# A decoder step on one core: convolution taps taken first, the convolution's scaling taken beside the input projection, three more weight tiles kept longer

## The chip, the cores and the metric

One Trainium2 chip, of which the kernel uses one core. The metric is the time of the device in microseconds (us). The profile is one execution on the chip; its rows name the engines: PE (matrix products), PEld (their weight loads), DVE (element by element), ACT (functions and copies), POOL (which here mostly issues transfers) and SP (which only issues transfers).

## The reference

One layer of a decoder trunk over 320 tokens (256 of a prompt, 8 sequences of 8 samples), in float32. Only what lies around the change is kept:

```python
ada = jax.nn.silu(c) @ w_ada + b_ada                 # (9, 2048) @ (2048, 12288)
sh1, sc1, g1, sh2, sc2, g2 = jnp.split(ada[:, None, :], 6, axis=-1)
h = _layer_norm(x) * (1.0 + sc1) + sh1
proj = h @ w_in                                      # (320, 2048) @ (2048, 7168)
u_s  = proj[..., :1024]                              # input of the S5 scan
u_c2 = proj[..., 1024:3072]                          # a * sigmoid(b): input of the convolution
gates = jax.nn.sigmoid(proj[..., 3072:])
y_s = S5 scan of u_s, then GELU, then two products (w_s5_val, w_s5_gate)
v = depthwise convolution, 31 taps, of a * sigmoid(b)
v = silu(_layer_norm(v, conv_ln_g, conv_ln_b)) @ w_conv_pw
x = layer_norm(alpha * x + g1 * ((g_s * y_s + g_c * v) @ w_out)); then the mixture of experts
```

## The kernel before

**Matrix products in three parts.** A weight is read in float32 into a tile `raw` (4 buffers of 128x1024, 512 KB each), and `split` makes of it `whi` (ACT, a rounding cast, L555) and `wlo` (DVE, `raw - whi`, L556). PE then multiplies `whi` with the high and the low part of the activations and `wlo` with the high part (`mm3`). A `gemm` makes 256 columns of the output in chunks of 512 KB of weights; one chunk is 24 matmuls of 320 columns (`acc<-h_hi,whi`, `acc<-h_lo,whi`, `acc<-h_hi,wlo`).

**The stages.** First `w_ada`, 1024 columns at a time (`ada_set`), which has the nine condition vectors `scT` as stationary operand; each step is a group of four matmuls that read two tiles, written `adp<-raw,scT` or `adp<-rawu,scT`. Four sets must be done before `h` is; beside them the layer norm of `x` and `s5_setup`, the tables of the S5 scan and small constants, go on, and `k_outer` begins the input projection's first 768 columns. Next the rest of the input projection: 2 x 4 gemms for the convolution's input (`ev_ua`, `ev_ub`) and then 16 gemms for the gates (`ev_g`), 64 chunks. Then `w_conv_pw` in 16 chunks (`acc<-vhl,whi`), the two products of the S5 branch, `w_out`, and the experts.

**What is done beside.** After every chunk `run_main` gives its side generators a budget: 2100 ns to the S5 scan `s5()` and 1700 ns to `conv()` followed by `conv_norm()`, and one step of the other `w_ada` sets (`ada_rest`). A generator's `yield` says what its piece costs. The convolution runs on PE as matmuls over `wide` (taps spread to a diagonal) and leaves `vf`; `conv_norm` sums `vf` and the squares (matmuls with `ones`), and makes the factor `rs` with `rstd_` (L318 to L324: a square root on ACT, a reciprocal and four more steps on DVE). `conv_out` multiplies `vf` by it (L910), takes silu (L911) and splits the result into `vhl` (L914, L915), which is the right operand of the `w_conv_pw` product. What is left of `conv_norm`, and all of `conv_out`, is run off between the last gate chunk and the first chunk of `w_conv_pw`.

**Weight tiles.** `ada_load` puts every other tile of `w_ada` into one of three extra tiles, `rawu` (two, in the buffer that `vf` takes later) and `rawc` (in the one that `wide` takes later), as long as the list `more` is not empty; `more.clear()` (L637) ends that before the last four `k_outer`. All loads of weights go through SP's queue in program order; a load waits there until its tile is free. S5's operands `Bs`, `us` and the convolution's windows `up_d` go through POOL's queue.

**Taps.** In `s5_setup` the weights of the convolution (31x1024) are brought from columns to rows by 128 small matmuls (`tpp<-kc,cwn`) that share the only `tpp` buffer of PSUM with all transposes.

The order of instructions on each engine is made by a scheduler that goes by data, buffers and priorities.

Of the kernel before, what the change touches and what calls it, by code (L numbers as in the profile page):

```python
# [9 lines left out]
F32 = mybir.dt.float32  # L10
F32R = mybir.dt.float32r
# [3 lines left out]
OP = mybir.AluOpType  # L15
AX = mybir.AxisListType.X
# [8 lines left out]
T = SEQ + NB * TS  # L25
NS = 1 + NB
DS = 1024
# [4 lines left out]
CW = 31  # L32
# [120 lines left out]
def build(tc, A, O):  # L153
    nc = tc.nc
    V, S, GP, PE, SY = nc.vector, nc.scalar, nc.gpsimd, nc.tensor, nc.sync
# [16 lines left out]
    cmr2, pr2 = pool(name="pr2", bufs=1, side="right")  # L172
    cma, pa = pool(name="pa", bufs=1)
# [7 lines left out]
    def tpp(name="tpp"):  # L181
        return pp.tile([128, 512], F32, name=name, tag="tpp", bufs=1)
# [4 lines left out]
    def mm(out, l, r, a, b, skip=True):  # L187
        return PE.matmul(out, lhsT=l, rhs=r, start=a, stop=b, skip_group_check=skip)  # L188

    tt, ts, stt = V.tensor_tensor, V.tensor_scalar, V.scalar_tensor_tensor  # L190
# [5 lines left out]
    ident = kc[:, C_ID:C_ID + 128]  # L196
# [12 lines left out]
    cwS = p0.tile([128, 8, 4, 8], F32, name="cwS", tag="cwT")  # L209
# [28 lines left out]
    def x_load():  # L238
        for i, (t0, n) in enumerate(TOK):
            if i < 2:  # L240
                SY.dma_start(out=xt[i], in_=A["x_prompt"][0, t0:t0 + n])
            else:
                SY.dma_start(out=xt[i][:n], in_=A["x_sample"].rearrange("b s d -> (b s) d"))
# [4 lines left out]
    ps = tpp()  # L248
# [81 lines left out]
    def ln0():  # L330
        st = stg("st")
        mv = stg("mv")
        for i, (t0, n) in enumerate(TOK):
            for c in range(4):
                V.bn_stats(st[:n, 24 * i + 6 * c:24 * i + 6 * c + 6], xt[i][:n, 512 * c:512 * c + 512])
            V.bn_aggr(mv[:n, 2 * i:2 * i + 2], st[:n, 24 * i:24 * i + 24].rearrange("p (c s) -> p c s", s=6))
            rstd_(mv[:n, 2 * i + 1:2 * i + 2], mv[:n, 16 + i:17 + i], mv[:n, 8 + i:9 + i])
            ts(xt[i][:n], xt[i][:n], mv[:n, 2 * i:2 * i + 1], mv[:n, 8 + i:9 + i], op0=OP.subtract, op1=OP.mult)

            stt(mv[:n, 24 + i:25 + i], mv[:n, 2 * i + 1:2 * i + 2], ALPHA, mv[:n, 8 + i:9 + i],  # L340
                op0=OP.mult, op1=OP.mult)
        yield
        for k in range(KT):
            ps = s5p()
            for i, (t0, n) in enumerate(TOK):
                PE.transpose(ps[:, t0:t0 + n], xt[i][:n, 128 * k:128 * k + 128], ident[:n, :n])
            S.copy(xnT[k // 8][:, k % 8, :], ps[:, :T])
            yield
        ps = tpp()
        for i, (t0, n) in enumerate(TOK):  # L350
            mm(ps[:, t0:t0 + n], bc(mv[:n, 24 + i:25 + i], [n, 128]), ident[:n, :n], True, True)
        V.tensor_copy(sdb, ps[:, :T])
        yield
# [35 lines left out]
    def s5_setup():  # L389
# [129 lines left out]
        ps = tpp()  # L519
        PE.transpose(ps[:, :64], vn[:64, :128], ident[:64, :64])  # L520
        V.tensor_copy(vT, ps[:, :64])
        cwn = pr2.tile([32, DS], F32, name="cwn", tag="Wb")
        GP.dma_start(out=cwn[:CW], in_=A["conv_w"][0])
        ps = tpp()
        pick = ident[:CW, 0:32].rearrange("p (r s) -> p s r", s=4)
        for c in range(8):
            for j in range(4):
                x = 32 * c + 8 * j
                for s in range(4):
                    mm(ps[32 * s:32 * s + 32, x:x + 8], cwn[:CW, 128 * c + 32 * j:128 * c + 32 * j + 32], pick[:, s, :],  # L530
                       True, True)
            yield 350
        V.tensor_copy(cwS.rearrange("p c j r -> p (c j r)"), ps[:, :256])
        V.tensor_reduce(oneh, ident.rearrange("p (a c) -> p c a", a=4), axis=AX, op=OP.add)
        yield 700

        h0 = p0.tile([128, 2, NB, NQ], F32, name="h0", tag="h0")
# [26 lines left out]
    def gemm(wv, c0, nk, xh, xl, evac):  # L564

        pss = []

        def load(k0):
            raw = raw_tile()
            SY.dma_start(out=raw.rearrange("p (k m) -> p k m", k=4), in_=wv[:, k0:k0 + 4, c0:c0 + 256])  # L570
            return split(raw, 1024)

        def prod(k0, hi, lo):
            if not pss:
                pss.extend(acc() for _ in range(2))
            for k4 in range(4):
                k = k0 + k4
                for m in range(2):
                    c = 256 * k4 + 128 * m
                    mm3(pss[m][:, :T], hi[:, c:c + 128], lo[:, c:c + 128], xh(k), xl(k), k == 0, k == nk - 1)  # L580
            if k == nk - 1:
                for m in range(2):
                    evac(c0 // 128 + m, pss[m][:, :T])

        for k0 in range(0, nk, 4):
            yield load, prod, k0
# [24 lines left out]
    def k_outer(k):  # L611
# [4 lines left out]
        for m in range(6):  # L616
            mm3(first[m][:, :T], hi[:, 128 * m:128 * m + 128], lo[:, 128 * m:128 * m + 128],
                hh[0](k), hh[1](k), k == 0, k == KT - 1)

    setup, norm = Side(s5_setup()), ln0()  # L620
    for q in range(4):
        for i, _ in enumerate(ada_set([D + 512 * q, 512 * q])):
            if q == 0:
                if i == 2:
                    x_load()
                if i == 3:
                    bias_rows()
                    next(norm)
                if 6 <= i < 15:
                    next(norm, None)  # L630
                    next(norm, None)
                setup.give(800)
            else:
                if i % 4 == 3 and i < 16:
                    k_outer(4 * q - 4 + i // 4)
                setup.give(1100)
    more.clear()  # L637
    for k in range(12, 16):
        k_outer(k)
    setup.flush()  # L640
# [209 lines left out]
    vv = {}  # L850
# [26 lines left out]
                yield 2000  # L877

    def conv_norm():
        yield 8000  # L880
        GP.dma_start(out=O["conv_p"][0, 0], in_=e_d[0:30])
        GP.dma_start(out=O["conv_s"][0, :, CW - 1 - TS:CW - 1], in_=e_d[30:94].rearrange("(b t) c -> b t c", b=NB))
        ps = s5p()
        for c in range(8):
            mm(ps[:, :T], ones, vf[:, c, :], c == 0, c == 7)
        yield 4000
        mu = stg("cmu")[:, :T]
        ts(mu, ps[:, :T], 1.0 / DS, None, op0=OP.mult)
        ps = s5p()
        for c in range(8):  # L890
            tt(vf[:, c, :], vf[:, c, :], mu, op=OP.subtract)
            sq = stg("csq")[:, :T]
            S.activation(sq, vf[:, c, :], AF.Square)
            yield 450
            mm(ps[:, :T], ones, sq, c == 0, c == 7)
        yield 1500
        va, tm = stg("cva")[:, :T], stg("ctm")[:, :T]
        rs = wide.rearrange("p j r x -> p (j r x)")[:, :T]
        ts(va, ps[:, :T], 1.0 / DS, None, op0=OP.mult)
        rstd_(va, tm, rs)  # L900
        yield 4500
        vv["rs"] = rs

    def conv_out():
        rs = vv["rs"]
        v_ = pa.tile([128, 2, 8, T], F32R, name="vhl", tag="H1")
        vv["hi"], vv["lo"] = v_[:, 0], v_[:, 1]
        for c in range(8):
            v = vf[:, c, :]
            tt(v, v, rs, op=OP.mult)  # L910
            S.activation(v, v, AF.Silu, bias=vT[:, 24 + c:25 + c], scale=vT[:, 16 + c:17 + c])  # L911
            yield 450
            hi, lo = vv["hi"][:, c, :], vv["lo"][:, c, :]
            S.copy(hi, v)  # L914
            tt(lo, v, hi.bitcast(F32), op=OP.subtract)  # L915
            yield 450

    ahead, due = [], []
# [1 line left out]
    def run_main(gens, sides=(), extra=None, before=None):  # L920


        def last():
            if ahead:
                prod, k0, hl, fn, sd, ev = ahead.pop()
                if fn:
                    fn()
                due.extend(later)
                later.clear()
                prod(k0, *hl)  # L930
                while due:
                    due.pop(0)()
                for x, ns in sd:
                    x.give(ns)
                if ev:
                    ev.give(1.0)

        for g in gens:
            for load, prod, k0 in g:
                hl = load(k0)  # L940
                last()
                ahead.append((prod, k0, hl, before, sides, extra))
                before = None
        if not gens:
            last()
# [29 lines left out]
            tt(x[o:o + 32], psg[r], x[r].bitcast(F32), op=OP.subtract)  # L975
        yield

    PACE = dict(s5=2100, conv=1700)
    def steps(g, cost):
        for _ in g:  # L980
            yield cost
# [13 lines left out]
    for i in range(4):  # L995
        run_main([gemm(w_in, 1024 + 256 * i, KT, *hh, ev_ua), gemm(w_in, 2048 + 256 * i, KT, *hh, ev_ub)], SD, ada_rest,
                 (lambda: side.g.append(s5())) if i == 0 else None)
    run_main([gemm(w_in, 3072 + 256 * i, KT, *hh, ev_g) for i in range(16)], SD, ada_rest,
             lambda: cside.g.extend((conv(), conv_norm())))


# [1280 lines left out]
```

## Time and profile before

| | us |
|---|---|
| median of 3 runs (1692.36 to 1695.34) | 1693.14 |
| the profiled execution | 1690.03 |
| its span | 1688.2 |
| PE busy | 1483.2 (88%) |
| DVE busy | 881.6 (52%) |
| ACT busy | 552.8 (33%) |
| mean granted clock of PE | 0.94 |

The stages in the trace: `w_ada` and setup 0 to 157 us, the first columns of the input projection to 179, the convolution's input and the gates to 708, `w_conv_pw` to 813, S5's products and `w_out` to about 1200, the experts to the end. Busy times are sums over an engine's instructions; what counts for the change is where PE stands idle and who ends that.

### The profile page before, as it was taken

What the parts mean: (1) busy time and instruction counts of PE and PEld (TensorE: products, weight loads), DVE (VectorE), ACT (ScalarE), POOL (GpSimd) and SP (SyncE); (2) the same over time, 40 slices, a digit from 0 to 9 for tenths busy, and PEclk for the clock granted to TensorE, in tenths of its full rate; (3) what the DMA queues carried; (4) which work ended last, traced back from release to release, by engine and by line L of the source; (5) the groups of instructions that cost most, each with busy time, mean ns of one, the idle gap of its engine ahead of it and who ended that gap; (6) DMA issues with size and microseconds to landing.
All of it is one profiled execution on the core that took longest, in us unless ns stands there. A gap on an engine that the chain in (4) does not pass through costs nothing. (4 is left out here: it accounts for less than half of the span.)

```text
span 1688.2 us, 28087 instructions
## 1 busy us (share of the span) xinstructions
PE 1483.2 (88%) x10731; PEld 1029.6 (61%) x10731; DVE 881.6 (52%) x1724; ACT 552.8 (33%) x960; POOL 248.6 (15%) x419
## 2 busy tenths in 40 slices
PE   4767988998998899949999999989889998969894
PEld 1444877877786777838899988848423332323331
DVE  5744347666744853695455554463531533424365
ACT  1312433342243234333343433331222423232434
POOL 3021312123223322011100000000200000010013
PEclk9887989999999999979999999988979999989997
DMA  9896999789688886637776645465799799999992
GB/s 287 273 340 221 283 276 240 232 222 260 183 251 202 207 235 206 183 126 235 242 255 221 210 136 170 154 231 208 293 406 412 299 412 402 412 365 412 412 410 73
DMA packets 214899, 447.39 MB, mean 265 GB/s; under 512 B 23811, under 2 KB 134067, under 8 KB 206732
## 3 DMA queue, kind: packets, MB, share of 16 engines
q1 hardware_dynamic: 179572, 395.65, 67.5%
q0 software_dynamic: 29168, 43.15, 11.1%
q10 hardware_dynamic: 6016, 6.70, 1.3%
q8 instruction: 87, 1.43, 0.4%
q14 instruction: 56, 0.46, 0.1%
HBM read 425.53 MB, written 21.77 MB: 265 GB/s over the span
## 5 line engine op out<-in xcount | busy, mean ns | idle before, releaser
L556 DVE TENSOR_TENSOR wlo<-raw,whi 128x1024 fp32r<-128x1024 f32 (+1 forms) x196 | 239.5, 1222 | 313.3 <-ACT whi L555 302.7
L555 ACT CAST whi<-raw 128x1024 fp32r<-128x1024 f32 (+1 forms) x196 | 201.9, 1030 | 419.7 <-PE acc L188 244.8
L188 PE MATMUL acc<-h_hi,whi 128*128 128x320 f32 x864 | 275.5, 322 | 14.0 <-ACT whi L555 11.7
L188 PE MATMUL acc<-h_lo,whi 128*128 128x320 f32 x864 | 272.3, 317 | 0.0
L188 PE MATMUL acc<-h_hi,wlo 128*128 128x320 f32 x864 | 259.0, 320 | 7.4 <-DVE wlo L556 7.1
L188 PEld LDWEIGHTS acc<-h_hi,whi 128*128 128x128 f32 x864 | 166.8, 194 | 41.3 <-ACT whi L555 21.3
L188 PE MATMUL up<-ring,xg 128*32 128x512 f32 x1344 | 181.6, 621 | 7.4 <-PEq L2197 6.5
L188 PEld LDWEIGHTS acc<-h_hi,wlo 128*128 128x128 f32 x864 | 161.8, 194 | 27.3 <-DVE wlo L556 13.2
L188 PEld LDWEIGHTS acc<-h_lo,whi 128*128 128x128 f32 x864 | 167.3, 194 | 2.6 <-issue 2.1
L188 PE MATMUL adp<-raw,scT 128*32 128x512 f32 x672 | 117.2, 673 | 31.5 <-DMA raw<-in_w_ada 31.4
L188 PEld LDWEIGHTS up<-ring,xg 128*32 128x32 f32 x1344 | 43.2, 115 | 100.4 <-issue 85.2
L188 PE MATMUL pd<-ring,aT 128*32 128x512 f32 (+1 forms) x688 | 98.2, 679 | 5.9 <-DVE aT L1870 5.9
L1708 DVE TENSOR_TENSOR x1tok<-x1tok,acc 128x512 f32<-128x512 f32 x80 | 51.8, 684 | 62.7 <-PE acc L188 62.4
L1926 ACT COPY z<-pd 32x512 f32<-32x512 f32 (+1 forms) x92 | 53.1, 577 | 89.0 <-PE pd L188 85.3
L188 PE MATMUL acc<-m_hi,whi 128*128 128x320 f32 x256 | 81.4, 319 | 0.0
L188 PE MATMUL acc<-m_lo,whi 128*128 128x320 f32 x256 | 80.0, 314 | 0.0
L188 PE MATMUL acc<-y_hi,whi 128*128 128x320 f32 x256 | 79.0, 311 | 0.0
L188 PE MATMUL acc<-y_lo,whi 128*128 128x320 f32 x256 | 78.6, 309 | 0.0
L188 PE MATMUL acc<-m_hi,wlo 128*128 128x320 f32 x256 | 78.2, 317 | 0.0
L188 PE MATMUL acc<-y_hi,wlo 128*128 128x320 f32 x256 | 74.7, 311 | 0.0
L188 PE MATMUL acc<-vhl,whi 128*128 128x320 f32 x256 | 57.3, 318 | 13.3 <-ACT vhl L914 12.9
L1609 DVE COPY xg<-XS 128x512 f32 x34 | 14.5, 428 | 81.2 <-PE up L188 78.4
(689 smaller groups left out, 2554.6 us busy)
## 6 DMA issues: line engine op xcount, KB each, us to landing
raw<-in_w_ada SPq DMA_DIRECT2D x128, 512.0 KB, 5.4
ring<-in_moe_w_up SPq DMA_DIRECT2D x120, 512.0 KB, 11.3
ring<-in_moe_w_gate SPq DMA_DIRECT2D x120, 512.0 KB, 10.5
ring<-in_moe_w_down SPq DMA_DIRECT2D x60, 1024.0 KB, 11.3
raw<-in_w_in SPq DMA_DIRECT2D x100, 512.0 KB, 4.9
raw<-in_w_ada SPq DMA_DIRECT2D x80, 256.0 KB, 5.5
raw<-in_w_out SPq DMA_DIRECT2D x32, 512.0 KB, 4.5
rawu<-in_w_ada SPq DMA_DIRECT2D x32, 256.0 KB, 5.4
```

The costliest lines, as they stand in the source:

```text
L188: return PE.matmul(out, lhsT=l, rhs=r, start=a, stop=b, skip_group_check=skip)
L555: S.copy(hi[:, :n], raw_ap)
L556: tt(lo[:, :n], raw_ap, hi[:, :n].bitcast(F32), op=OP.subtract)
L1609: state[g % 2] = (V.tensor_copy if g % 2 == 0 else S.copy)(xg[:, :, 32 * g:32 * g + 32], XS[:, :, bass.ds(off, 32)])
L1708: tt(x, x, o, op=OP.add)
L1926: S.copy(zs[q * ng + nb][0][s0:s0 + m_], pd[m_ * q:m_ * q + m_])
```

## The change

Three edits. The load of the convolution's weights and the 128 small matmuls on them leave `s5_setup` and stand in a function `taps()`, called at the third step of the first `w_ada` set; their tile is one of the `whi` buffers instead of the `Wb` buffer. `more.clear()` stands after the eight gemms `ev_ua`, `ev_ub`, so that `ada_rest` uses the three extra tiles there. The multiplication by `rs` and the silu go from `conv_out` to the end of `conv_norm`, whose first `yield` is 3000 instead of 8000, and the convolution's side is given 1900 instead of 1700 per chunk.

```diff
@@ s5_setup
-        cwn = pr2.tile([32, DS], F32, name="cwn", tag="Wb")
-        GP.dma_start(out=cwn[:CW], in_=A["conv_w"][0])
-        ps = tpp()
-        pick = ident[:CW, 0:32].rearrange("p (r s) -> p s r", s=4)
-        for c in range(8):
...
-            yield 350
-        V.tensor_copy(cwS.rearrange("p c j r -> p (c j r)"), ps[:, :256])
-        V.tensor_reduce(oneh, ident.rearrange("p (a c) -> p c a", a=4), axis=AX, op=OP.add)
@@ before the first ada_set
+    cwn = pa.tile([32, DS], F32, name="cwn", tag="whi", bufs=2)
+    GP.dma_start(out=cwn[:CW], in_=A["conv_w"][0])
+    def taps():
+        ps = tpp()
...
                 if i == 2:
                     x_load()
+                    taps()
...
-    more.clear()
     for k in range(12, 16):
         k_outer(k)
@@ conv_norm
-        yield 8000
+        yield 3000
...
         rstd_(va, tm, rs)
         yield 4500
-        vv["rs"] = rs
-
-    def conv_out():
-        rs = vv["rs"]
-        v_ = pa.tile([128, 2, 8, T], F32R, name="vhl", tag="H1")
-        vv["hi"], vv["lo"] = v_[:, 0], v_[:, 1]
         for c in range(8):
             v = vf[:, c, :]
             tt(v, v, rs, op=OP.mult)
             S.activation(v, v, AF.Silu, bias=vT[:, 24 + c:25 + c], scale=vT[:, 16 + c:17 + c])
             yield 450
-            hi, lo = vv["hi"][:, c, :], vv["lo"][:, c, :]
-            S.copy(hi, v)
-            tt(lo, v, hi.bitcast(F32), op=OP.subtract)
+
+    def conv_out():
+        v_ = pa.tile([128, 2, 8, T], F32R, name="vhl", tag="H1")
+        vv["hi"], vv["lo"] = v_[:, 0], v_[:, 1]
+        for c in range(8):
+            S.copy(vv["hi"][:, c, :], vf[:, c, :])
+            tt(vv["lo"][:, c, :], vf[:, c, :], vv["hi"][:, c, :].bitcast(F32), op=OP.subtract)
             yield 450
@@
-    PACE = dict(s5=2100, conv=1700)
+    PACE = dict(s5=2100, conv=1900)
@@ main loop
     for i in range(4):
         run_main([gemm(w_in, 1024 + 256 * i, ...ev_ua), gemm(w_in, 2048 + 256 * i, ...ev_ub)], SD, ada_rest, ...)
+    more.clear()
     run_main([gemm(w_in, 3072 + 256 * i, KT, *hh, ev_g) for i in range(16)], SD, ada_rest,
              lambda: cside.g.extend((conv(), conv_norm())))
```

**Place 1: the taps.** PE's order at the end of the `w_ada` stage of before: transposes for the S5 tables (L507, L520), the taps, two and one more groups on `w_ada`, and the first product on `h`.

```order
L507 MATMUL tpp<-kc,cN 128x128 x4
L520 MATMUL tpp<-kc,misc 128x64
L188 MATMUL tpp<-kc,cwn 32x8 x128
L188 MATMUL adp<-rawu,scT 32x512
L188 MATMUL adp<-raw,scT 32x512 x2
L188 MATMUL adp<-rawu,scT 32x512
L188 MATMUL adp<-rawc,scT 32x512
L188 MATMUL adp<-raw,scT 32x512 x2
L188 MATMUL adp<-rawc,scT 32x512
L546 MATMUL tpp<-kc,misc 128x128 x4
L188 MATMUL adp<-raw,scT 32x512 x4
L188 MATMUL tpp<-pair,ae 128x64 x8
```

The same place after the change (L533 is L546 of before); the taps are gone and the groups on `w_ada` stand one by one between the transposes, and half of `tpp<-pair,ae` goes ahead of the last group.

```order
L507 MATMUL tpp<-kc,cN 128x128 x4
L188 MATMUL adp<-rawu,scT 32x512
L188 MATMUL adp<-raw,scT 32x512 x2
L188 MATMUL adp<-rawu,scT 32x512
L507 MATMUL tpp<-kc,cN 128x128 x4
L520 MATMUL tpp<-kc,misc 128x64
L533 MATMUL tpp<-kc,misc 128x128 x4
L188 MATMUL adp<-rawc,scT 32x512
L188 MATMUL adp<-raw,scT 32x512 x2
L188 MATMUL adp<-rawc,scT 32x512
L188 MATMUL tpp<-pair,ae 128x64 x4
L188 MATMUL adp<-raw,scT 32x512 x4
```

PE's order at the beginning of the program after the change, from its fourth row; in before the rows without `cwn` stood there alone. 18 of the taps now stand between the first and the second group on `w_ada`, and 110 between the second and the third.

```order
L188 MATMUL adp<-rawu,scT 32x512
L188 MATMUL adp<-raw,scT 32x512 x2
L188 MATMUL adp<-rawu,scT 32x512
L397 MATMUL tpp<-kc,misc 128x96
L188 MATMUL tpp<-kc,cwn 32x8 x18
L188 MATMUL adp<-rawu,scT 32x512
L188 MATMUL adp<-raw,scT 32x512 x2
L188 MATMUL adp<-rawu,scT 32x512
L188 MATMUL tpp<-kc,cwn 32x8 x110
L188 MATMUL adp<-rawc,scT 32x512
L188 MATMUL adp<-raw,scT 32x512 x2
```

**Place 2: from the gates to `w_conv_pw`.** PE's order of before, from the last matmul of the gates on.

```order
L188 MATMUL acc<-h_hi,wlo 128x320
L188 MATMUL s5p<-csq,ones 128x320 x5
L188 MATMUL tpp<-pair,ae 128x64 x4
L188 MATMUL adp<-raw,scT 32x512 x4
L188 MATMUL s5p<-csq,ones 128x320 x3
L188 MATMUL adp<-raw,scT 32x512 x8
L188 MATMUL acc<-vhl,whi 128x320 x2
L188 MATMUL py<-s5S,Cl 32x320
```

PE's order after the change at the same place; the sums over `csq` stand some 280 to 310 rows earlier, between gate chunks, and one group on `w_ada` is left between the two products.

```order
L188 MATMUL acc<-h_hi,wlo 128x320
L188 MATMUL adp<-raw,scT 32x512 x4
L188 MATMUL acc<-vhl,whi 128x320 x3
L188 MATMUL acc<-vhl,wlo 128x320
L188 MATMUL acc<-vhl,whi 128x320
```

ACT's order after the change in the last ten gate chunks (L542 is the cast L555 of before, L760 a copy of the S5 scan, L907 the silu L911 of before, L319 the square root); in before L319 and L911 stood behind the last cast of a gate chunk.

```order
L319 ACT_TABLE_LOAD
L319 ACTIVATE ctm<-cva 128x320
L542 CAST whi<-raw 128x1024
L760 COPY Wre<-s5p 128x5x64
L760 COPY Wim<-s5p 128x5x64
L542 CAST whi<-raw 128x1024
L760 COPY Wre<-s5p 128x5x64
L760 COPY Wim<-s5p 128x5x64
L907 ACT_TABLE_LOAD
L907 ACTIVATE vf<-vf,vT 128x320 x2
L542 CAST whi<-raw 128x1024
```

**Place 3: the loads of weights.** SP's order of before, from the last loads of `k_outer` (L614) into the chunks for the convolution's input (L570); then that after the change (L601, L557). Of every pair of tiles of `w_ada` (L279) one now goes to an extra tile, for nine of the first twelve pairs; the order of the loads is the same.

```order
L614 DMA raw<-in_w_in 128x768 x5
L570 DMA raw<-in_w_in 128x4x256 x6
L279 DMA raw<-in_w_ada 128x1024 x2
L570 DMA raw<-in_w_in 128x4x256 x2
L279 DMA raw<-in_w_ada 128x1024 x2
L570 DMA raw<-in_w_in 128x4x256 x3
```

```order
L601 DMA raw<-in_w_in 128x768 x5
L557 DMA raw<-in_w_in 128x4x256 x6
L279 DMA raw<-in_w_ada 128x1024
L279 DMA rawu<-in_w_ada 128x1024
L557 DMA raw<-in_w_in 128x4x256 x2
L279 DMA raw<-in_w_ada 128x1024
L279 DMA rawu<-in_w_ada 128x1024
L557 DMA raw<-in_w_in 128x4x256 x3
```

After the twelfth pair the two orders read alike.

## Rows read from the trace of the kernel before

**Rows 1.** Stretch, length; busy us of PE, PEld, DVE, ACT, POOL; clock, DMA share, GB/s.

```profile
708.00:813.50 105.50, 80.24 (x508) 65.67 (x511) 77.51 (x150) 36.75 (x55) 15.14 (x30) 0.87 0.55 182
730.00:740.00 10.00, 0.00 (x0) 0.00 (x0) 10.00 (x17) 0.00 (x0) 2.44 (x5) 0.50 0.51 170
```

**Rows 2.** PE in order of time, 700 to 815: start, duration, operation, [idle before <-releaser].

```profile
700.88 4.47 PE L188 MATMUL s5p<-vf,ones 128*128 128x320 f32 x16
...
707.82 0.31 PE L188 MATMUL acc<-h_lo,whi 128*128 128x320 f32 x1
707.97 0.31 PE L188 MATMUL acc<-h_hi,wlo 128*128 128x320 f32 x1
...
727.25 1.94 PE L188 MATMUL adp<-raw,scT 128*32 128x512 f32 x8 [5.93 <-DMA raw<-in_w_ada]
742.12 0.90 PE L188 MATMUL acc<-vhl,whi 128*128 128x320 f32 x2 [12.93 <-ACT vhl L914]
745.52 1.24 PE L188 MATMUL py<-s5S,Cl 128*32 128x320 f32 x2 [2.50 <-DVE s5S L816]
...
751.42 0.41 PE L188 MATMUL acc<-vhl,whi 128*128 128x320 f32 x1
...
813.41 1.06 PE L188 MATMUL adp<-raw,scT 128*32 128x512 f32 x8
```

**Rows 3.** DVE in order of time, 721 to 740.

```profile
721.15 0.49 DVE L899 TENSOR_SCALAR cva<-s5p 128x320 f32<-128x320 f32 x1
...
726.06 2.15 DVE L320 RECIPROCAL wide<-ctm 128x320 f32<-128x320 f32 x1 [1.31 <-ACT ctm L319]
...
739.99 3.31 DVE L910 TENSOR_TENSOR vf<-vf,wide 128x320 f32<-128x320 f32 x8
```

**Rows 4.** ACT in order of time, 724 to 726.

```profile
724.20 1.28 ACT L319 ACT_TABLE_LOAD   x1 [8.34 <-DVE cva L318]
725.49 0.47 ACT L319 ACTIVATE ctm<-cva 128x320 f32<-128x320 f32 x1
725.98 1.28 ACT L699 ACT_TABLE_LOAD   x1
```

**Rows 5.** Costliest groups of the whole run: busy, mean ns of one, idle before.

```profile
L556 DVE TENSOR_TENSOR wlo<-raw,whi 128x1024 fp32r<-128x1024 f32 (+1 forms) x196 | 239.5, 1222 | 313.3 <-ACT whi L555 302.7
```

**Rows 6.** PE in order of time, 141 to 154.

```profile
141.19 1.13 PE L188 MATMUL tpp<-kc,cwn 31*32 31x8 f32 x115 [0.32 <-DVE vT L521]
142.67 1.89 PE L188 MATMUL tpp<-kc,cwn 31*32 31x8 f32 x128 [0.35 <-issue]
147.77 0.39 PE L188 MATMUL tpp<-kc,cwn 31*32 31x8 f32 x13 [3.21 <-issue]
148.09 1.06 PE L188 MATMUL adp<-rawu,scT 128*32 128x512 f32 x1
...
153.41 1.07 PE L188 MATMUL adp<-raw,scT 128*32 128x512 f32 x8 [0.64 <-DMA raw<-in_w_ada]
```

**Rows 7.** SP's loads in order of time: issue, time taken by the issues.

```profile
138.92 12.00 SPq L279 DMA_DIRECT2D raw<-in_w_ada  x4
151.82 13.92 SPq L614 DMA_DIRECT2D raw<-in_w_in  x5
```

**Rows 8.** All engines in one stretch, columns as in rows 1.

```profile
144.00:152.00 8.00, 4.79 (x74) 1.70 (x67) 0.42 (x1) 0.00 (x0) 0.08 (x1) 0.50 0.31 102
```

**Rows 9.** PE in order of time, about 29 us.

```profile
29.43 1.06 PE L188 MATMUL adp<-rawc,scT 128*32 128x512 f32 x1 [10.64 <-DMA rawc<-in_w_ada]
```

**Rows 10.** PE's waits, 179 to 330 us (total, times, longest).

```profile
PE acc L188 <- ACT whi L555: 6.8, 2, 6.4
```

**Rows 11.** All engines in one stretch, columns as in rows 1.

```profile
184.00:232.00 48.00, 38.83 (x238) 35.15 (x237) 21.67 (x25) 16.50 (x29) 15.41 (x27) 0.89 1.11 305
```

**Rows 12.** PE's waits from 330 to 705 us.

```profile
PE adp L188 <- DMA raw<-in_w_ada: 16.3, 3, 6.2
```

**Rows 13.** POOL's transfers just before the first of these waits.

```profile
399.95 0.74 POOL L863 DMA_DIRECT2D s5S<-up_d  x1 [2.38 <-DMA Bs<-B_d]
```

More of the change, by code (lines that the diff above doesn't have):

```diff
@@ L521, in s5_setup @@
         V.tensor_copy(vT, ps[:, :64])
-        cwn = pr2.tile([32, DS], F32, name="cwn", tag="Wb")
-        GP.dma_start(out=cwn[:CW], in_=A["conv_w"][0])
-        ps = tpp()
-        pick = ident[:CW, 0:32].rearrange("p (r s) -> p s r", s=4)
-        for c in range(8):
[L527 to L531, printed above, removed]
-            yield 350
-        V.tensor_copy(cwS.rearrange("p c j r -> p (c j r)"), ps[:, :256])
-        V.tensor_reduce(oneh, ident.rearrange("p (a c) -> p c a", a=4), axis=AX, op=OP.add)
         yield 700
@@ L618, in k_outer @@
                 hh[0](k), hh[1](k), k == 0, k == KT - 1)
+    cwn = pa.tile([32, DS], F32, name="cwn", tag="whi", bufs=2)
+    GP.dma_start(out=cwn[:CW], in_=A["conv_w"][0])
+    def taps():
+        ps = tpp()
+        pick = ident[:CW, 0:32].rearrange("p (r s) -> p s r", s=4)
+        for c in range(8):
+            for j in range(4):
+                x = 32 * c + 8 * j
+                for s in range(4):
+                    mm(ps[32 * s:32 * s + 32, x:x + 8], cwn[:CW, 128 * c + 32 * j:128 * c + 32 * j + 32], pick[:, s, :],
+                       True, True)
+        V.tensor_copy(cwS.rearrange("p c j r -> p (c j r)"), ps[:, :256])
+        V.tensor_reduce(oneh, ident.rearrange("p (a c) -> p c a", a=4), axis=AX, op=OP.add)
     setup, norm = Side(s5_setup()), ln0()
@@ L912, in conv_out @@
             yield 450
-            hi, lo = vv["hi"][:, c, :], vv["lo"][:, c, :]
-            S.copy(hi, v)
-            tt(lo, v, hi.bitcast(F32), op=OP.subtract)
+    def conv_out():
+        v_ = pa.tile([128, 2, 8, T], F32R, name="vhl", tag="H1")
+        vv["hi"], vv["lo"] = v_[:, 0], v_[:, 1]
+        for c in range(8):
+            S.copy(vv["hi"][:, c, :], vf[:, c, :])
+            tt(vv["lo"][:, c, :], vf[:, c, :], vv["hi"][:, c, :].bitcast(F32), op=OP.subtract)
             yield 450
```

## The prediction, made before the changed kernel ran

> **What bounds the kernel now.** I read the page first: PE is busy for most of the span and DVE for about half of it, so PE's order of work sets the time and what can be won is where PE stands still. Then the windows, stage by stage, to find where it does. The worst place lies between the gates and `w_conv_pw`: from 708 to 813.5 PE works 80.2 of 105.5 us at a mean clock of 0.87, and between 730 and 740 not at all while DVE is busy for the whole of it [rows 1]. Then PE's timeline of that place, for who ends each wait: 5.93 us for a tile of `w_ada`, 12.93 for `vhl`, 2.50 for the S5 scan [rows 2]. The other places are the last groups on `w_ada` about 142 to 154 [rows 6] and 6.8 us of waits for `whi` between 179 and 330 [rows 10]. From 330 to 705 PE waits three times for a tile of `w_ada`, 16.3 us together [rows 12]. The experts are not touched.
>
> Waits cost more than their length, for the clock falls in them: the same group on `w_ada` takes 1.94 us at 727.25, after a wait, and 1.06 at 813.41 [rows 2]; 0.50 in rows 1 is the level of 1.2 GHz, 1.00 that of 2.4.
>
> I make the sum against the profiled execution, 1690.0 us, of which the span is 1688.2. The median of the runs stands 3.1 us above it, and I add that at the end. About 0.2%, 3.4 us, is what a measurement here can tell from no change.
>
> **Part 1, the convolution's norm.** Before, everything from the mean's subtraction on is run off while PE has nothing else. The chain is one of DVE and ACT: the variance at 721.15, the reciprocal 726.06 to 728.2, the scaling of `vf` from 739.99 [rows 3]. Between the reciprocal and the scaling DVE is never idle, yet the norm has only four small steps there; the S5 scan's pieces stand between them. So 708.28 (707.97 + 0.31) to 813.41, when the last group in front of the S5 products starts, is 105.1 us [rows 2].
>
> After the change the sums over `csq` stand some 280 to 310 rows of PE's order before the last gate matmul, and only one group on `w_ada` stands between the products. What this stretch then costs:
> - From 751.42 to 813.41 PE of before has full work at the full clock: 62.0 us [rows 2]. That stays.
> - 14 matmuls of `w_conv_pw` were already done in the slow part, and so were the 16 small ones for `py`, which I put at the 1.2 us that the row of the first two shows: 14 x 0.15 (the distance of the two matmuls at 707.8) + 1.2 = 3.3 [rows 2].
> - Of the three groups on `w_ada` in the stall one now goes ahead into the gates and two stay behind the last gate matmul; each 1.06 [rows 2]. With the sums over `csq` (as many matmuls of that shape as the sum over `vf`, 4.47 us [rows 2]) and the transposes `pair,ae` (about 1) that is 3 x 1.1 + 4.5 + 1 = 8.8 us of work which is still paid, somewhere.
> - New waits in the gates. The path from the variance over square root, reciprocal and the next `wlo` is 724.20 to 728.2 and one split of 1.22 [rows 3 to 5], some 5.2 us, against which PE has one split chunk ahead, 24 x 0.15 = 3.6: I take 1.5, between 0 and 5 (three table loads of 1.28 [rows 4] and the eight scalings of 3.31 [rows 3] both meet splits, and nothing is left ahead).
> - At the boundary `vhl` still has to be made: cast and subtraction of the first slices, between 0.5 and 3; I take 1.5.
> - DVE. In this stretch it worked 77.5 us [rows 1]. The norm's part that leaves is the subtraction and the scaling, about 3.3 each [rows 3], and reciprocal with its neighbours, some 4.7 (2.15 and five steps of about 0.5): 66 us stay, against about 75 of PE. It no longer gets the free 30 us, so `py` may wait for the scan (2.50 at 745.52 [rows 2]): I take 2.5, between 0 and 8.
>
> The sum is 62.0 + 3.3 + 8.8 + 1.5 + 1.5 + 2.5 = 79.6, so 25.5 us are won; with all lower bounds 31, with all upper ones 15.
>
> **Part 2, the taps.** Before, the taps hold PE from 141.19 to 148.09, and the transposes after them `tpp` [rows 6]. Meanwhile SP stands at a load of `w_ada` for 12.0 us, since its tile waits for a group behind the taps [rows 7]; from 144 to 152 DMA is used to 0.31, and the clock is 0.50 [rows 8]. So the 6.9 us are on the path, and slots come back late. The last group starts at 153.41 after a wait of only 0.64 [rows 6], and `h` needs it. With the taps gone PE takes these groups when their tiles land: won are 6.9 and a part of the half clock behind it, 8 in sum; between 4 (the loads, which had been stopped, then end the stage) and 10.
>
> In the new place they are 6.9 us of PE work between the first three groups. PE waits 10.64 us there for a tile [rows 9], and 110 of the 128 stand in that very gap; their load is 31 rows of 4 KB and the first in POOL's queue. I cost this at nothing; if the load landed late it would hold the second group on `w_ada`, at most 6.9.
>
> **Part 3, more tiles.** From 179 to 330 the waits for `whi` are 6.8 us, one of 6.4 [rows 10], and the half clock after it costs some 3 more (24 matmuls of 0.15 at 1.94 / 1.06 of their time [rows 2]). With every other tile of `w_ada` in an extra tile, the four `raw` tiles go to `w_in` more often and its loads are issued earlier. That helps only if the tile is late for want of a slot and not of bandwidth; from 184 to 232 the DMA share is already 1.11 [rows 11]. Between 0 and 10; I take 5, the middle. `wide` takes its buffer only when `rawc` is free, which the order puts before the convolution's first matmuls: nothing.
>
> **The sum:** 25.5 + 8 + 5 = 38.5, 1690.0 - 38.5 = 1651.5, and with 3.1 for the median 1654.6: 1655 us.
>
> **The rivals.**
> *The norm's chain bites in the gates.* Its table loads, reciprocal and scalings stand in the queues of ACT and DVE in front of casts and splits that PE needs within 3.6 us, and the scan that had 30 us of DVE for itself now runs beside `w_conv_pw`. Against it: on average a chunk needs only 1.22 us of DVE and the scan 2.1. With the upper bounds of part 1 it is 15 instead of 25.5, so 1665.
> The Trainium skill ("ScalarE: Activation LUTs", section "What ACT_TABLE_LOAD costs") puts a change of function set at a load of about 1.28 us and a drain of about 1.38, 2.66 together. The rows bear out the load alone: 1.28, the square root 1.29 after it, and the next load 0.02 behind the square root's end [rows 4]. Three changes in the gates would be 8.0 by the page and 3.8 by the rows; if none of the difference were covered the time would be some 4 us later, 1659.
> *The loads bound the early stages.* DMA ends both the `w_ada` stage and the chunks after it: the taps then give 4 and the tiles nothing. For it: the DMA share of 1.11 from 184 to 232 [rows 11]. Against: 0.31 in rows 8 and 12.0 us of SP's standing. 25.5 + 4 is 1664.
> *The other side: the convolution's faster pace meets S5's loads.* Three times a group on `w_ada` waited 5 to 6 us, as S5's operands `Bs`, `us` and the convolution's `up_d` came through POOL's queue together [rows 12, 13]; each costs some 5.4 and about 3 at half clock behind it, 8.5. At a pace of 1900 the convolution's 16 blocks shift against S5's. Five more such meetings eat all that is won: 1690 - 38.5 + 42.5 + 3 = 1697. Against it: the order of POOL has three such meetings after the change as well, not eight.
>
> **How the numbers follow.** Forecast 0.63 (own range 1645 to 1662); the norm's chain 0.14; the loads 0.13; the other side 0.04; 0.06 remain for a gain above the bounds, below 1645. Between 1638 and 1675 lie the forecast, nearly all of the first two rivals and most of that last case. Faster by over 0.2% is all but the other side and a little of the two rivals: 0.92; within it 0.04; slower 0.04.
>
> **What would show it.** Right: the first `acc<-vhl` starts within 3 us after the last gate matmul and its group on `w_ada`, at the full clock, and from the end of the gates to the first group of the S5 products it is about 71 us (79.6 without the 8.8, and with two groups on `w_ada`, less the 1.5 in the gates) instead of 105.1; no `cwn` row about 141 and the last group of the `w_ada` stage at about 146; the taps in a wait before 30 us. Wrong: waits for `wlo` or `whi` above 3 us in the last twelve gate chunks; a `py` that waits 5 us or more and brings the half clock; the third group on `w_ada` later than at 29.4 [rows 9]; more than three waits of 5 us for `w_ada` from 330 on; an unchanged 6.4 us wait about 222. The prediction falls if the gain at the norm is below 15.

## The result and the profile after

The changed kernel takes 1677.5 us (median of 4 runs, 1671.1 to 1680.6) against 1694.2 of before (1692.4 to 1698.0): 0.989 of before, 95% interval 0.986 to 0.991. It is 17 us faster; 39 were forecast, and the time lies above the range. The profiled execution took 1679.3 us, its span is 1677.5.

Five marks on PE say where the time went: R, when the groups on `w_ada` first run at the full rate after 30 us; A, the last matmul of the first four `w_ada` sets (its group starts 0.5 to 0.9 us earlier); B, the 1076th of the 2688 records of products on `h` (40%, about where the gates begin); C, the last gate matmul; D, the first matmul of the S5 products. All are starts in us, read from PE's timeline.

| profile of | R | A | B | C | D | end |
|---|---|---|---|---|---|---|
| before | 33.5 | 153.9 | 339.9 | 708.0 | 814.4 | 1688.2 |
| changed | 65.5 | 157.2 | 341.9 | 719.0 | 807.7 | 1677.5 |

So the `w_ada` stage got 3 us longer instead of 8 shorter (PE's next product on `h` starts at 157.8 instead of 157.5, since in before sixteen transposes `pair,ae` stood between A and it), A to B went from 186.0 to 184.7, the gates (B to C) from 368.1 to 377.1, C to D from 106.4 to 88.7, and all behind D from 873.8 to 869.8. The sum is the 10.7 us between the two spans; the medians are 17 apart. One profile of each is a rough measure: of the 10.7, 7.9 lie behind the first `w_out` matmul (748.3 and 740.4 us), a stretch that no run here edits and that takes from 737 to 748 us in the 20 profiles of this document.

The boundary itself is what was forecast. PE's timeline of the changed kernel, from the gates into the S5 products:

```profile
718.90 0.31 PE L188 MATMUL acc<-h_lo,whi 128*128 128x320 f32 x1
...
797.02 1.06 PE L188 MATMUL adp<-raw,scT 128*32 128x512 f32 x8
798.02 0.33 PE L844 MATMUL tpp<-kc,h 128*128 128x128 f32 x1
800.80 0.33 PE L844 MATMUL tpp<-kc,h 128*128 128x128 f32 x1 [2.46 <-DVE fe L846]
807.72 0.61 PE L188 MATMUL acc<-y_hi,whi 128*128 128x320 f32 x1 [6.59 <-DVE m L1010]
```

The last gate matmul starts at 719.0, and the group in front of the S5 products, which stood at 813.41 [rows 2], starts at 797.0: 78 us instead of 105. But then PE waits 2.46 and 6.59 us, where before it went on at once, and the first product after it runs at half rate. The same place in before, where the two transposes stand inside the `w_conv_pw` product:

```profile
805.03 0.27 PE L842 MATMUL tpp<-kc,h 128*128 128x128 f32 x1
808.37 0.27 PE L842 MATMUL tpp<-kc,h 128*128 128x128 f32 x1
...
814.41 0.41 PE L188 MATMUL acc<-y_hi,whi 128*128 128x320 f32 x1
```

Whom PE waits for after the change is in DVE's timeline and, one step on, in POOL's:

```profile
800.46 0.28 DVE L846 COPY fe<-tpp 128x128 f32<-128x128 f32 x1
801.17 0.29 DVE L846 COPY fe<-tpp 128x128 f32<-128x128 f32 x1 [0.42 <-PE tpp L844]
807.09 0.49 DVE L1010 TENSOR_TENSOR m<-gc,acc 128x320 f32<-128x320 f32 x1 [5.63 <-DMA gc<-gt_d]
```

```profile
796.14 0.52 POOL L841 DMA_DIRECT2D out_im_p<-fe  x1 [2.82 <-DVE fe L840]
801.04 0.56 POOL L847 DMA_DIRECT2D out_im_s<-fe  x1 [4.38 <-DVE fe L846]
801.59 2.13 POOL L1009 DMA_DIRECT2D gc<-gt_d  x4
```

POOL's timeline of before at the same loads:

```profile
805.92 0.55 POOL L845 DMA_DIRECT2D out_im_s<-fe  x1 [3.29 <-DVE fe L844]
806.48 2.14 POOL L1008 DMA_DIRECT2D gc<-gt_d  x4
```

The last four loads of gate values `gc` stand in POOL's queue behind a store of S5's last states, `out_im_s`, before and after. The store waits for a copy of DVE, and that for a transpose that PE of the changed kernel reaches only behind the last `w_conv_pw` matmul; in before it was done at 805.03, 8.4 us ahead of the group. Without `gc` the product's PSUM tiles are not emptied, and the S5 products have none to write to.

In the gates the waits for loads of `w_ada` and of windows changed their name, and their sum went from 17.1 (16.3 and 0.8) to 21.1. PE's waits from 345 to 722 in the changed kernel, which answer to rows 12 (16.3 us of groups on `w_ada`):

```profile
PE cv L188 <- DMA s5S<-up_d: 14.0, 6, 4.4
PE adp L188 <- DMA raw<-in_w_ada: 7.1, 4, 3.7
PE s5p L188 <- DMA us<-u_d: 1.1, 1, 1.1
PE acc L188 <- DVE wlo L543: 0.7, 1, 0.7
```

Of the norm's chain itself there is hardly a wait there: 0.7 us for `wlo`.

Beside the convolution's input the one wait of 6.4 us [rows 10] is gone, and several for `w_ada` stand in its place; the DMA share from 184 to 232 is 1.11 as in rows 11 (waits from 179 to 330, then the window, of the changed kernel):

```profile
PE adp L188 <- DMA rawc<-in_w_ada: 5.1, 2, 4.2
PE acc L188 <- DVE wlo L543: 4.4, 4, 1.8
PE adp L188 <- DMA raw<-in_w_ada: 3.1, 1, 3.1
PE adp L188 <- DMA rawu<-in_w_ada: 2.5, 2, 2.3
PE acc L188 <- DVE ul L649: 1.9, 1, 1.9
PE acc L188 <- ACT whi L542: 1.2, 1, 1.2
```

```profile
184.00:232.00 48.00, 42.44 (x274) 37.84 (x273) 22.38 (x26) 17.42 (x30) 15.34 (x27) 0.97 1.11 320
```

And at the start, the changed kernel's PE timeline shows the taps in their new place and what comes behind them:

```profile
19.59 2.42 PE L188 MATMUL tpp<-kc,cwn 31*32 31x8 f32 x166
28.01 0.92 PE L188 MATMUL tpp<-kc,cwn 31*32 31x8 f32 x54 [6.00 <-issue]
30.68 1.06 PE L188 MATMUL adp<-rawc,scT 128*32 128x512 f32 x1 [1.75 <-DMA rawc<-in_w_ada]
...
52.78 4.64 PE L346 MATMUL s5p<-kc,xt 128*128 128x128 f32 x15
57.35 1.93 PE L188 MATMUL adp<-raw,scT 128*32 128x512 f32 x8
```

The third group comes at 30.7 (29.4 in rows 9; a later one was named as a sign of being wrong, but this is 1.3 us), so nearly all of the taps is hidden there as such. But at 57.35 a group still takes 1.93 us, the half rate, and fifteen transposes 4.64. A group of before, ten us earlier:

```profile
46.55 1.07 PE L188 MATMUL adp<-raw,scT 128*32 128x512 f32 x8
```

The first product on `h` starts at 71.9 us, with one group on `w_ada` more in front of it than in before; there it was 57.8, with the full rate from 33.5 on.

### The profile page after: what moved, and what is told of

It is laid out like the page before. It is cut to its first block, busy times and chain, and to the rows that moved or that the text cites. A ratio compares the mean times of both kernels' runs of the same rounds, so it can differ in the third digit from the quotient of the medians.

```text
span 1677.5 us, 28072 instructions
## 1 busy us (share of the span) xinstructions
PE 1486.2 (89%) x10731; PEld 1039.7 (62%) x10731; DVE 878.0 (52%) x1724; ACT 550.3 (33%) x960; POOL 247.6 (15%) x419
## 3 DMA queue, kind: packets, MB, share of 16 engines
q1 hardware_dynamic: 179572, 395.65, 67.8%
## 5 line engine op out<-in xcount | busy, mean ns | idle before, releaser
L542 ACT CAST whi<-raw 128x1024 fp32r<-128x1024 f32 (+1 forms) x196 | 201.8, 1030 | 388.6 <-PE acc L188 231.9
L188 PE MATMUL up<-ring,xg 128*32 128x512 f32 x1344 | 175.5, 610 | 11.1 <-DMA ring<-in_moe_w_gate 10.2
L188 PE MATMUL adp<-raw,scT 128*32 128x512 f32 x636 | 120.7, 689 | 22.9 <-DMA raw<-in_w_ada 22.9
```

Source lines behind the costliest of these rows:

```text
L542: S.copy(hi[:, :n], raw_ap)
```

## Experiments

Medians are told with the ratio to the runs of before on the same chip and its 95% interval. Single runs of before lay between 1682 and 1707 us over these chips, so the ratios are the better comparison.

**The parts alone.** Each of the three edits was made in before without the other two, as the diff shows them. The fourth run is the changed kernel with S5's last states put behind the `w_conv_pw` product:

```diff
 # s5(): its last loop becomes a generator s5_tail()
     run_main([gemm(w, 256 * i, 8, *yy, ev) for i in range(8) for w, ev in (...)],
-             SD, ada_rest, side.flush)
+             SD, ada_rest, lambda: (side.flush(), side.g.append(s5_tail())))
```

Taps alone: 

> Before, with the taps moved alone. Theory (the move sets PE to work at half rate between the first groups on w_ada, and the gain at 141 us is given back there): within 4 us of before; the group on w_ada at about 40 us takes 1.9 instead of 1.06, and the first product on h comes at about 72 instead of 58 us. Rival (the taps gain what was forecast and the loss is that of another part): 6 to 9 us faster than before.

1693.5 us, 0.999 (0.996 to 1.002). No gain that can be told from nothing, and the forecast's 8 us (0.995) lie just outside of the interval; the 6 at the rival's lower end do not. The groups at 35 to 50 us take 1.9, R is 55.4, the first product on `h` starts at 68.2 (not 72), and A is 154.0 as in before. The theory's time holds; that the half rate is what takes the gain back is not shown by it.

Extra tiles alone: 

> Before, with the three extra tiles kept for eight gemms more, alone. Theory (bandwidth bounds that stretch, so the wait of 6.4 us at 222 is cut into several): within 4 us of before. Rival: 5 us faster, as forecast.

1693.2 us, 1.002 (0.999 to 1.006); A to B is 185.7 against 186.0, and the longest wait for `whi` there is 4.3 instead of 6.4. The theory's size holds.

Scaling and pace alone: 

> Before, with the convolution's scaling moved and its pace 1900, alone. Theory: 13 to 20 us faster: about 27 won from the gates' end to the end of the w_conv_pw product, of which some 10 go to a wait for gate values (gc) behind stores of S5's last states, and some more to waits for the convolution's windows in the gates. Rival (the norm gave what was forecast and the early parts took it back): 25 us faster.

1678.4 us, 0.990 (0.986 to 0.994): 14 us, as much as the whole change gives within the intervals. C to D is 86.1, with the same wait for `gc` in front of the S5 products (7.1 us). The theory holds.

Later states: 

> The changed kernel, with the transposes and stores of S5's last states (the end of s5) taken beside the S5 products instead of the w_conv_pw product, so that no load of gate values stands behind a store. Theory: the 9 us that PE waits before the S5 products go, 7 to 10 us faster than the changed kernel. Rival (the loads are late for another reason, or the states then delay the S5 products): within 3 us of the changed kernel.

1672.0 us, 0.987 (0.982 to 0.991). The changed kernel had 0.989 on its own chip, so this is some 4 us by the ratios, within the intervals; against the scaling alone (e3), on the same chip, it is 6 us, and the intervals overlap there too. The theory had 7 to 10, so the time decides nothing, but the trace does. PE's timeline of this run shows the wait gone; the S5 products follow at once and at the full rate, and C to D is 76.8 instead of 88.7:

```profile
796.38 1.07 PE L188 MATMUL adp<-raw,scT 128*32 128x512 f32 x8
797.37 0.41 PE L188 MATMUL acc<-y_hi,whi 128*128 128x320 f32 x1
```

**Places of the taps, and the windows' lead.** These four have the scaling, its pace and the later states, and the tiles as in before. The taps are called at `i == 0` of the first set (taps first) or at `q == 1, i == 1` (second set). The lead is

```diff
-                yield 3500
+                yield 3900
                 ps, lead = s5p("cv"), None
...
-                yield 2000
+                yield 1600
```

Without the taps' move: 

> The move of the scaling with its pace and the later states of S5; taps and extra tiles as before. Theory (taps and tiles give nothing): the same as the run with all of them, within 5 us of 1672; PE at the full rate from 37 us on. Rival (they help, hidden by the spread): 1680.

1675.0 us, 0.986 (0.983 to 0.988), like the run with taps and tiles; R is 33.4, A 156.8.

Taps first: 

> As the run with the scaling and the later states, with the taps earlier still: before and after the first group on w_ada, so that PE is idle from 20 to 29 us again. Theory A (taps in the long wait just before the third group hold the clock's rise back): the clock rises near 36 us, h begins near 58, and the taps' place at 141 us is free: 3 to 8 us faster than the run without them. Theory B (taps anywhere before 30 us do it): the half rate lasts to 55 us or longer and the time is the same as without.

1666.7 us, 0.981 (0.978 to 0.985). That is 8 us less than without the move, on the same chip, the size of theory A and of the forecast, and A (152.7) and B (342.0) are both 4 us earlier. But theory A's way there isn't seen: R is 50.3, between the two, and `h` begins at 67.7.

Taps in the second set: 

> As the run with the scaling and the later states, with the taps in the second set of w_ada, at about 50 us. Theory (the half rate belongs to the place before 30 us): the clock rises near 36 us, the taps run at full rate beside waits for w_ada, 141 us is free: 3 to 8 us faster. Rival (the w_ada stage ends when its bytes are there, whatever stands on PE): the same time as without, within 3 us, with the last group on w_ada at the same time.

1675.2 us, 0.985 (0.981 to 0.988). R is 37.5, as the theory has it, and A is 149.1, 7.7 us earlier than without the move. But the time is the same: A to B takes 197.0 instead of 188.9, so all of it is given back there.

Three chunks of lead: 

> As the run with the scaling and the later states, with the convolution's two yields 3900 and 1600 instead of 3500 and 2000, so that three chunks instead of two lie between the issue of its windows and their use at 1900 per chunk. Theory (at the new pace the windows are late by their landing time): the waits of cv for up_d, about 10 us, fall under 2 and the time by 5 to 12. Rival (the same bytes meet anyway, and the wait goes back to the groups on w_ada, as in before): the sum of both waits stays within 4 us, and so does the time.

1673.8 us, 0.987 (0.982 to 0.992). The rival: `cv` still waits 10.6 us for `up_d`, groups on `w_ada` 6.3, together 16.9 against 18.2 without the longer lead. So the lead is not what makes the windows late; that it is bytes that meet is argued.

**All together, and its bounds.** All edits of the change, the later states and the taps first; then that with `conv=1700`; then, at 1900 again, with fewer steps on `w_ada` beside the convolution's input:

```diff
-    def steps(g, cost):
-        for _ in g:
-            yield cost
+    def steps(g, cost, n=0):
+        for i, _ in enumerate(g):
+            yield 1.9 if i < n else cost
...
-                                  for p in (2, 4, 3) for i in range(2)]), 1.3))
+                                  for p in (2, 4, 3) for i in range(2)]), 1.2, 17))
```

> All of it: the scaling and its pace, the later states of S5, the extra tiles, and the taps around the first group on w_ada. Theory (the taps' gain of about 5 us in the w_ada stage is given back before 236 us by loads that are late, unless w_ada has tiles of its own): 1665, as the run without the extra tiles or some us less; from the first product on h past the first w_ada sets to 40% of the input projection's matmuls about 180 us. Rival (the extra tiles only move the wait): the same time as without them, with that stretch at 184.

1671.1 us, 0.985 (0.980 to 0.990), no better than the 0.981 without the tiles (e6, on another chip). A to B is 185.0 against 189.4 without them, but A came at 160.3 and R at 65.4, 8 and 15 us later than in e6, on the same PE instructions in the same order up to 150 us. So this run can't price the tiles.

> The run with all of it, with the convolution's pace put back to 1700. Theory (at 1900 the windows have two chunks to land instead of three, and cv waits for them): the waits of cv for up_d fall from about 10 to 2 us, the groups on w_ada wait about 16 us again as in before, and since the norm then ends only at the last gate chunk some 3 to 8 us appear before the first vhl: the same to 8 us slower. Rival (the pace itself costs the 8 us that the gates are longer): 5 us faster.

1678.8 us, 0.989 (0.985 to 0.994), 8 slower than at 1900. The waits went back as the theory has it:

```profile
PE adp L188 <- DMA raw<-in_w_ada: 16.4, 4, 6.7
PE acc L188 <- DVE wlo L543: 2.1, 1, 2.1
```

B to C is 378.1 against 375.3, so the pace costs the gates nothing, and C to D is 88.5 against 79.7: at 1700 the norm isn't done in time (its scaling starts at 732.7, 9 us behind C). The faster pace belongs to the gain.

> The run with all of it, with fewer steps on w_ada beside the convolution's input (a cost of 1.9 instead of 1.3 for the first 17 steps, then 1.2), so that 9 instead of 11 pairs of tiles load there. Theory (bytes, not slots, bound that stretch): it gets 5 to 10 us shorter, and the gates get some of it back; 0 to 6 us faster in all. Rival (slots or DVE bound it): the stretch stays within 2 us.

1659.7 us, 0.978 (0.974 to 0.983), 11 less. A to B falls from 185.0 to 175.7, of which 2 are two groups on `w_ada` that now come later, and the gates take 4.2 us more. PE's waits for `w_ada` from 160 to 345 fall from 11.4 to 3.4. So the stretch gets shorter where fewer bytes are asked for, as the theory has it. But A itself came 10 us earlier (150.0 against 160.3, with R at 43.6 instead of 65.4), ahead of the first step that the edit changes. In the profiles that is the larger part, so the 11 us are not the price of the bytes alone.

**Taps and tiles again, where bytes bound less.** On one chip, five rounds: the kernel of the last run again (f3), with the taps at the old place (f1), with the taps at the change's place (f2), and with the tiles given back as in before (f4).

> The fastest version (scaling and pace, later states, extra tiles, fewer steps on w_ada beside the convolution's input), with the taps at their old place in s5_setup. Theory (the taps held the w_ada stage for about 4 us, the bytes do the rest): 3 to 6 us slower than the two with the taps moved. Rival A (forecast: 8 us on the path): 8 us slower. Rival B (the stage is as long as its bytes): the same within 2 us.

> The fastest version with the taps at the place of the change (18 after the first group on w_ada, 110 after the second). Theory (half rate till 55 us or longer costs nothing that the loads don't cost anyway): the same as with the taps around the first group, within 3 us. Rival (the half rate there takes back what the taps give): like the version with the taps at the old place.

> The fastest version again, with the taps around the first group on w_ada, beside its two sisters: 1660 by the run before, 0.978 of before.

> The fastest version with the extra tiles given back before the convolution's input, as in before. Theory (with fewer bytes of w_ada in that stretch the slots matter even less): the same within 3 us. Rival (the tiles are worth the forecast 5 us once bytes don't bound): 5 us slower.

| | median us | ratio (interval) | R | A | A to B |
|---|---|---|---|---|---|
| f1 taps at the old place | 1665.3 | 0.982 (0.978 to 0.986) | 36.7 | 156.7 | 186.0 |
| f2 taps as in the change | 1656.3 | 0.977 (0.972 to 0.981) | 43.0 | 152.5 | 173.8 |
| f3 taps first | 1656.1 | 0.976 (0.972 to 0.980) | 44.3 | 151.0 | 174.5 |
| f4 tiles given back | 1670.2 | 0.984 (0.980 to 0.989) | 64.6 | 157.6 | 188.2 |

My theory for f4 falls, and that for f1 is too small. Here the taps' move is worth 9 us (1665.3 - 1656.2), what the forecast had, at either place, and the kernel without the tiles is 14 us slower. With both, A to B is 174; without either one it is 186 to 188, as long as in before. So these edits are no terms that add up. The taps' move was worth 0 at the change's place in before (e1), 8 at the first step with neither tiles nor fewer bytes (e6), 0 in the second set (e7), and 9 here. The tiles were worth 0 in before (e2). How much of the 14 is theirs isn't shown, for f4 is late already ahead of the place where they act. f2 and f3 beat before and the changed kernel, by 39 and 21 us.

**The late full rate.** In f4, A is 6.6 us later than in f3, with the same work up to there but R at 64.6 instead of 44.3. The same holds for e9 against e11. That asks whether R is chance. One more profile each of the changed kernel, of all together, and of f3:

> The changed kernel once more, for one profile. Theory A (the moment at which PE's rate rises after the taps is chance of the execution): it differs from the 65 us of its first profile, and the last group of the first four sets on w_ada comes at 150 to 153 if it is below 51, at 157 to 160 if it is above 60. Theory B (it belongs to the kernel): 62 to 66 us again and the last group at 157.

> The run with all of it and the taps around the first group, once more, for one profile. Theory A (chance): a rise other than at 65 us in this or one of the two beside it, and the last group follows it. Theory B (kernel): 65 us again and the last group at 160.

> The fastest version once more, for one profile; its first 160 us are the instructions of the run beside it. Theory A (chance): any of the two. Theory B (kernel): 44 us again, the last group at 150 to 151.

Single times 1678.9, 1669.9 and 1650.4 us (before 1693.1). R is 65.0, 67.8 and 44.0, where the first profiles had 65.5, 65.4 and 44.3; A is 155.3, 158.3 and 150.6. So it belongs to the kernel rather than to the execution, by one repetition of each.

## Why the prediction was wrong, by its steps

**Part 1, the norm: the mechanism right, one wait missed.** 78 us from the gates' end to the group in front of the S5 products, where the prediction had about 71; the gates took 9.0 more (6.6 of work and 1.5 of waits were forecast there, for two of the three groups on `w_ada` were to stay behind them). In the 78 are waits of 2.1 for `vhl`, 2.7 for `wlo` and 0.9 for `w_ada`, where 4.0 were forecast (`vhl` and `py`; `py` didn't wait), and two spells of half rate:

```profile
719.00:730.00 11.00, 8.17 (x45) 6.80 (x44) 11.00 (x29) 5.63 (x12) 0.00 (x0) 0.84 0.66 220
740.00:750.00 10.00, 7.30 (x40) 6.06 (x38) 10.00 (x15) 2.10 (x2) 1.60 (x3) 0.83 0.46 152
```

What failed is the list of what is late next: it named `vhl`, `py` and splits, followed no queue behind the end of the product, and so had no wait in front of the S5 products. The loads of `gc` had always stood behind S5's stores. Now PE came to the group in front of the S5 products 16 us earlier (797.0 against 813.4) and these loads only 5 us earlier (801.6 against 806.5), and they became the end of the chain: 9.1 us of waits, and the products on `y` ran at half rate for a while (D to the first `w_out` matmul 129.4 us instead of 125.6). So 25.5 became 14 (e3), which is below the 15 at which the prediction said that it falls. e4 shows that this wait goes with the order of the stores: C to D 76.8.

**Part 2, the taps: right about the old place, wrong about what it is worth.** The two steps that failed are "won are 6.9 and a part of the half clock behind it" and "I cost this at nothing": 8 were forecast, and the move alone gave 0 (e1). As PE work the taps are hidden; but in this kernel PE works at half rate until 65.5 us instead of 33.5, the layer norm's transposes and the groups on `w_ada` take twice as long, and A is at 157.2 instead of about 146. Over the 20 profiles, kernels with the taps in the first set and R below 51 have A at 150 to 153, those with R above 60 at 155 to 160, and e1 between them (55.4) has 154. But those with the taps at the old place, with R at 33 to 37 in all six and the same PE instructions in the same order up to 150 us, have A anywhere from 154 to 159. So that the rate is the cause is argued from this order, not shown: no run changed the rate alone. Nor is it the only way to lose the gain: in e7 the rate rose at 37.5 and A came 7.7 us earlier, as forecast, and all of it was given back by B; in e6 the 4 us gained at A were kept. What decides this stays open.

**Part 3, the tiles: the doubt was right, the middle of the bounds was not.** The sentence that weighed slots against bandwidth had a row against the 5 us, a share of 1.11 [rows 11]; 5 was taken and 0 came (e2). Whether the tiles give more where fewer bytes are asked for is not settled by f4 against f3, for f4 also had the late rate.

**The rivals.** "The loads bound the early stages" is the nearest, with 1664 as its time; with the wait for `gc` (9.1 and the half rate after it) on top it comes to the measured time. A part of that is luck: it gave the taps 4 us, which e1 doesn't show, and its bound on bytes is borne out by e2 and in part by e11. The norm's chain did not bite in the gates: 0.7 us for `wlo`. By the Trainium skill ("ScalarE: Activation LUTs", section "What ACT_TABLE_LOAD costs") each change of function set has a drain of about 1.38 us beside its load. The changed kernel's trace shows none: the load follows the copy before it at once, and the silu stands 1.30 behind the load's start.

```profile
677.33 0.42 ACT L760 COPY Wim<-s5p 128x320 f32<-128x320 f32 x1 [0.16 <-PE s5p L188]
677.77 1.28 ACT L907 ACT_TABLE_LOAD   x1
679.07 1.20 ACT L907 ACTIVATE vf<-vf,vT 128x320 f32<-128x320 f32 x2
```

The other side didn't come either: waits for loads in the gates, `w_ada` and windows together, are 21 us instead of 17, none of those for `w_ada` is above 3.7, and the pace of 1900 is 8 us better than 1700 (e10). The reason given, groups of S5's loads that meet the windows, was right in kind: which engine operation waits went with the pace (e10). The sum of these waits lies between 9 (f1, with more of `w_ada` in the gates) and 21 (the changed kernel), so the bytes alone don't fix it.

**The measurement.** The bound of 0.2% was too fine: three rounds give intervals of 0.3 to 0.5% to either side.

## What to carry to other kernels

When PE is made to arrive earlier at a boundary, follow every in-order queue that feeds the next stage to its end: a load that stands behind a store is as late as the store's source, and it costs nothing until PE comes before it. Where the DMA share is as high as here (1.11), an edit that frees a slot or a few us of PE ahead of that stretch may be worth nothing by itself (e1, e2, e7) and something beside others (e6, f1 to f3); so try such edits again after each other, for what each is worth depends on the rest. And compare a stretch that nothing edits: it shows what one profile can tell.

## What was not expected of the hardware

PE worked at half rate for tens of us while it was busy without a gap, and the profile's clock column said 1.00. The window 40 to 56 us in all together (second profile) and in f3, and one row of each:

```profile
40.00:56.00 16.00, 16.00 (x62) 6.00 (x58) 3.52 (x22) 4.58 (x11) 0.00 (x0) 1.00 0.63 209
```

```profile
40.00:56.00 16.00, 15.98 (x102) 7.06 (x100) 5.90 (x18) 7.27 (x18) 0.00 (x0) 1.00 0.87 290
```

```profile
48.70 3.43 PE L346 MATMUL s5p<-kc,xt 128*128 128x128 f32 x11
```

```profile
48.62 2.95 PE L346 MATMUL s5p<-kc,xt 128*128 128x128 f32 x15
```

Eleven transposes in 3.43 us against fifteen in 2.95, 62 records in the window against 102, at the same clock column. The column is not a measurement there. It is the mean of the trace's clock entries and counts time without an entry as 1.00, and the first entry, of the full level, stands at 67.6 us in the first of these two kernels, at 41.6 in f3, at 65.3 in the changed kernel and at 33.4 in before: in all 20 profiles 0 to 3 us ahead of R. In before, too, the column says 1.00 from 24 to 32 us, while the group at 29.43 takes the time of the half rate [rows 9]:

```profile
24.00:32.00 8.00, 2.21 (x10) 0.48 (x11) 7.08 (x27) 0.56 (x3) 0.00 (x0) 1.00 1.02 331
```

And where the changed kernel has entries of 0.50, a group takes the same 1.94 us as in front of the first entry (1.93 at 57.35):

```profile
69.00:75.00 6.00, 4.94 (x19) 3.28 (x20) 6.00 (x11) 2.38 (x5) 0.00 (x0) 0.50 0.81 272
```

```profile
70.06 1.94 PE L188 MATMUL adp<-raw,scT 128*32 128x512 f32 x8 [3.45 <-DMA raw<-in_w_ada]
```

So PE is at the lower of its two levels, 1.2 GHz, from the program's start until its first rise, and R is that rise: 33.5 us in before, 43 to 68 in the kernels with the taps in the first set. Ahead of the first entry the duration of a known operation tells the rate, and the column does not. Both kernels above have the same instructions in the same order on PE up to there, and the moment of the rise came back within 2.4 us for each of the three kernels that were profiled again; what in a kernel sets it stays open.
